# Attention's buffers move to the other side of the on-chip memory, and its first tiles are issued beside the last of the input projection

## The chip, the cores and the metric

The kernel runs on one core of one Trainium2 chip. A core has five engines, each with its own list of instructions that it runs in order: PE (TensorE, matrix products), DVE (VectorE, elementwise work and reductions), ACT (ScalarE, table functions, copies and casts), POOL (GpSimd) and SP (SyncE, which here only issues loads and stores). Engines wait for one another through semaphores, and so does SP: a load that has to wait holds up every load and store behind it in SP's list. The data lie in an on-chip memory of 128 partitions (SBUF); products are summed in a small second memory (PSUM). Everything larger lies in the chip's main memory (DRAM), and loads and stores go through 16 DMA engines.

The metric is the device time of one execution in microseconds. The kernel before takes 3681.51 us, the median of three runs from 3678.64 to 3687.2.

## The reference

The reference is a backbone of two layers over 256 context tokens and 1024 latent tokens with 1024 features each. In every layer the normed tokens go through one input projection, whose columns feed four mixers of 256 features each; the mixers' outputs are put side by side and go through one output projection onto the residual stream; then comes a feed-forward network with 4096 hidden features.

```
z   = norm(x) * (1 + scale) + shift;  z @ W_in  -> S5 | mLSTM | attention | GLA
mix = concat(S5(..), mLSTM(..), attention(..), GLA(..))
x   = x + gate * (mix @ W_out)
x   = x + gate2 * (relu(norm2(x) @ W1)**2 @ W2)
```

Attention is differential: each of the four heads has two score maps of 32 features a query, `o = softmax(q0 k0) v - lambda * softmax(q1 k1) v` with 64 features in v, and an RMS norm over o. Latent queries see all 1280 keys, context queries only the 256 of the context. The last layer needs no context outputs.

## The kernel before

Each product in float32 is done as three matmuls on rounded halves (high by high, low by high, high by low; `mm3`). So every weight that arrives (`raw`) is split by ACT (`whi`, line 1119) and DVE (`wlo`, line 1120). One layer runs in this order, by the lines of the part that builds it:

- The input projection is a generator (`rest`, tiles `zp` in PSUM, `zst` on the way out to DRAM). Its steps are traced as filler beside the S5 mixer, then beside the GLA mixer (`beside(gla, rest, 1400)`), and what is left at the end of GLA is traced in one piece (`list(rest)`). `beside(main, filler, rate)` lets the filler advance by `rate` units for each step of main. In layer 0 the steps that make the modulation vectors (`later`) follow.
- Then the pools of the projection's input and weights (`hpc`, `wpc`) are shut. `p_out` (the generator `po`) is the half of the output projection that reads the outputs of S5 and GLA: per block of 256 tokens and each of 8 groups of rows, one product of 12 matmuls (`wop`), written with the residual to a DRAM tensor `xn`.
- `da_mix` (the generator `da`) is attention. Per head it loads four tiles `daqk` of 128 x 1280 numbers, once also `davt` (v). A pair of queries' tiles gives scores (`daps`, PE, line 488); DVE takes them out of PSUM and finds the maxima (`das`, line 489); ACT takes exponentials (line 500); DVE combines the two maps (line 508); PE turns the result over (`dapt`, line 529), ACT copies it out (`dawT`) and PE multiplies by v (`dapo`, line 520). At the end of a head there is a norm (`dapr`, `dao`, `dasq`, `dams`, lines 547 to 556) and a store `mix<-dao`. A step of `da` is a score tile, a transposed group or a group of products; layer 0 has 372 steps and layer 1 has 340.
- `ml_mix` (the generator `ml`) is the mLSTM, whose gates are found by `ml_gates`: it starts with small arithmetic and short round trips through DRAM (`ml_small`, `mlsb`, `ml_rows`, `mlE`), loads q, k and v, and runs a convolution over them (`mlcy`, lines 724 to 736); then come chunks. It has about 90 steps in layer 0 and 80 in layer 1.
- The three are traced together: `beside((1 for _ in both(da, 1, ml, 0.25)), po, 0.12)`: a quarter of an mLSTM step and 0.12 products of `po` for each step of attention. Then what is left of `ml` and of `po`.
- Then the residual stream is loaded back whole (`X<-xn`, 128 x 8 x 256 numbers for the context and 128 x 8 x 512 for each half of the latent tokens), and the second half of the output projection reads the outputs of mLSTM and attention (`mr<-mix`, cast to `mh` by ACT at line 1448 and to `ml` by DVE at line 1449; again tiles `wop`), adds into X (line 1530), and the feed-forward network follows (`m1p`, `m2p`).

What sets the order is a list scheduler: it gives each engine its instructions with the traced order as priority, and the engine then runs them as they stand. Memory is handed out in pools from two ends, left and right. A tile whose place was another's before waits until that one's last reader is done. Before, `da_mix` opens its pool `dam` on the left, on the place that the projection's input and weights had, so that its first load waits for the end of the projection; the mLSTM's pools `mlg` and `ml` lie on the right, where GLA's were. The residual's pool (`X`) and the weights' pool of the second half of the output projection (`wo`) are opened on the right.

Of the kernel before, what the change touches and what calls it, by code (L numbers as in the profile page):

```python
# [452 lines left out]
def da_mix(env, l, st, V, lamv, lam_init, normg, bones, out_cb, need_ctx):  # L453

    tc, nc = env.tc, env.nc
    v, g, act, pe = nc.vector, nc.gpsimd, nc.scalar, nc.tensor
    with tc.tile_pool(name=f"dam{l}", bufs=1, reuse_waits="tile") as P:
        vt = P.tile([128, 10, 256], F32, name="davt")  # L460
        def constants():
            lv = P.tile([128, 512], F32, tag="rs_u", name="lamv", bufs=1)[:, 0:128].rearrange("p (a b) -> p a b", a=4)
            nc.sync.dma_start(lv, lamv)
            ng = P.tile([128, 1], F32, name="ng")
            nc.sync.dma_start(ng, normg)
            v.tensor_scalar(ng, ng, 1.0 - lam_init, None, op0=ALU.mult)
            lp = P.tile([128, 2, 32], F32, name="lp")
            v.tensor_tensor(lp, lv[:, 0::2, :], lv[:, 1::2, :], op=ALU.mult)
            ls = P.tile([128, 2], F32, name="ls")
            v.tensor_reduce(ls, lp, axis=AX.X, op=ALU.add)  # L470
            le = P.tile([128, 2], F32, name="le")
            exp_exact(nc, P, le, ls, 2, "le")
            nlam = P.tile([128, 1], F32, name="nlam")
            v.tensor_tensor(nlam, le[:, 1:2], le[:, 0:1], op=ALU.subtract)
            v.tensor_scalar(nlam, nlam, -lam_init, None, op0=ALU.add)
            return ng, nlam

        def scores(Q, K, qt, k1, rs):
            S, sm = {}, {}
            late_at = 2  # L480
            npc = (k1 + 511) // 512
            for m in (1, 0):
                s = S[m] = P.tile([128, T], F32, tag="s%d" % m, name="das", bufs=4 - 2 * m)
                pm = P.tile([128, 4], F32, tag="pm", name="dapm", bufs=6)
                for i in range(npc):
                    a, b = 512 * i, min(k1, 512 * i + 512)
                    p = env.bank("das2" if i == 2 else "das", "daps")
                    pe.matmul(p[:, 0:b - a], Q[m][:, 128 * qt:128 * qt + 128], K[m][:, a:b], start=True, stop=True)  # L488
                    v.tensor_scalar(s[:, a:b], p[:, 0:b - a], -1.0, None, op0=ALU.mult, op1=ALU.min, accum_out=pm[:, i:i + 1])  # L489
                    if not late_at:  # L490
                        while late:
                            late.pop(0)()
                    late_at -= 1
                    yield 1
                nm = pm
                if npc > 1:
                    nm = P.tile([128, 1], F32, tag="nm", name="danm", bufs=6)
                    v.tensor_reduce(nm, pm[:, 0:npc], axis=AX.X, op=ALU.min)  # L498
                sm[m] = P.tile([128, 1], F32, tag="sm", name="dasm", bufs=6) if m else rs
                act.activation(s[:, :k1], s[:, :k1], AF.Exp, bias=nm[:, 0:1], scale=-1.0, accum_out=sm[m])  # L500
            tiles.append(S[0])

            def combine():

                r1 = P.tile([128, 1], F32, tag="rs", name="dars", bufs=6)
                v.reciprocal(r1, sm[1])
                v.tensor_scalar(r1, r1, nlam, sm[0], op0=ALU.mult, op1=ALU.mult)
                v.scalar_tensor_tensor(S[0][:, :k1], S[1][:, :k1], r1, S[0][:, :k1], op0=ALU.mult, op1=ALU.add)
            late.append(combine)
            while len(late) > 1:  # L510
                late.pop(0)()

        def values(SS, po, h, pi, k1):

            nk = k1 // 128

            def products(i, n, wT):
                for j in range(i, i + n):
                    for z in range(2):
                        pe.matmul(po[64 * z:64 * z + 64, 128 * pi:128 * pi + 128], vt[:, j, 64 * h:64 * h + 64], wT[z][:, j - i], start=j == 0, stop=j == nk - 1)  # L520
            before = None
            for i in range(0, nk, 4):
                n = min(4, nk - i)
                wT = []
                for S in SS:
                    w = P.tile([128, 4, 128], F32, tag="wT", name="dawT", bufs=4)
                    p = env.bank("dat", "dapt")
                    for j in range(n):
                        pe.transpose(p[:, 128 * j:128 * j + 128], S[:, 128 * (i + j):128 * (i + j) + 128], env.ident)  # L529
                    act.copy(w[:, 0:n].rearrange("p a b -> p (a b)"), p[:, 0:128 * n])  # L530
                    wT.append(w)
                    yield 1
                if before:
                    products(*before)
                    yield 1
                before = (i, n, wT)
            products(*before)
            yield 1

        def finish(po, h, pairs, rs):  # L540

            n = 128 * len(pairs)
            v.reciprocal(rs[:, 0:2 * len(pairs)], rs[:, 0:2 * len(pairs)])
            pr = env.bank("dat", "dapr")
            for pi in range(len(pairs)):
                for z in range(2):
                    pe.matmul(pr[64 * z:64 * z + 64, 128 * pi:128 * pi + 128], rs[:, 2 * pi + z:2 * pi + z + 1].to_broadcast([128, 64]), env.ident, start=True, stop=True)
            o = P.tile([128, 512], F32, tag="o", name="dao", bufs=1)[:, 0:n]
            act.copy(o, pr[:, 0:n])
            v.tensor_tensor(o, o, po[:, 0:n], op=ALU.mult)  # L550
            sq = P.tile([128, 512], F32, tag="rs_u", name="dasq", bufs=1)[:, 0:n]
            act.activation(sq, o, AF.Square)
            pms = env.bank("dat", "dams")
            pe.matmul(pms[:, 0:n], bones, sq, start=True, stop=True)
            y = rstd_wide(env, P, pms[:, 0:n], n)
            v.scalar_tensor_tensor(o, o, ng, y, op0=ALU.mult, op1=ALU.mult)
            for z in range(2):
                out_cb(h, o[64 * z:64 * z + 64, 0:n], 128 * pairs[0][z])
            yield 1
        tiles, late = [], []  # L560
        todo = []

        def drain(n):
            while n and todo:
                for _ in todo[0]:
                    n -= 1
                    yield 1
                    if not n:
                        return
                todo.pop(0)  # L570
        for h in range(4):
            Qs, Ks = [], []
            for hm in (2 * h, 2 * h + 1):
                for w, L_ in ((1, Ks), (0, Qs)):
                    tl = P.tile([128, T], F32R, tag="qk%d" % w, name="daqk%d" % w, bufs=3)
                    src = st[w].rearrange("b i (j h) t -> (b i j) h t", h=8)[:, hm, :]
                    c0 = 0 if need_ctx or w == 1 else TC
                    nc.sync.dma_start(tl[:, c0:].bitcast(F32), src[:, c0:])
                    L_.append(tl)
            if h == 0:  # L580
                ng, nlam = constants()
                nc.sync.dma_start(vt, V.rearrange("(t p) c -> p t c", p=128))
            for pairs, k1 in ([([(0, 1)], TC)] if need_ctx else []) + [([(2, 6), (3, 7), (4, 8), (5, 9)], T)]:
                po = env.bank("dao", "dapo")
                rs = P.tile([128, 8], F32, tag="rk", name="dark", bufs=2)
                for pi, pr in enumerate(pairs):
                    for z in range(2):
                        yield from scores(Qs, Ks, pr[z], k1, rs[:, 2 * pi + z:2 * pi + z + 1])
                        yield from drain(5 + z)
                    todo.append(values((tiles.pop(-2), tiles.pop()), po, h, pi, k1))  # L590
                todo.append(finish(po, h, pairs, rs))
        for f in late:
            f()
        yield from drain(1000)
# [513 lines left out]
DQ = 32 ** -0.5  # L1108
HID = (2, 4)


# [158 lines left out]
def tile_hybrid_backbone(ctx: ExitStack, tc: tile.TileContext, io, out):  # L1270
# [97 lines left out]
    for l in range(L):  # L1368
# [62 lines left out]
        if l == 0:  # L1431
            list(later)
            make_scale(0, 1)
# [283 lines left out]
```

## Time and profile before

| | before |
|---|---|
| median of three runs | 3681.51 us (3678.64 to 3687.2) |
| the profiled execution | 3686.26 us, its span 3684.5 us |
| busy share of the span: PE, DVE, ACT, POOL | 92%, 60%, 36%, 12% |
| TensorE's granted clock, mean | 0.955 |
| layer 0: last store of GLA; last matmul of the projection; first score tile | 601.89; 629.9; 648.14 us |
| layer 0: last store of attention; first product that reads it | 1006.51; 1015.78 us |
| layer 1: last store of GLA; last matmul of the projection; first score tile | 2530.77; 2560.5; 2571.09 us |
| layer 1: last store of attention; first product that reads it | 2882.68; 2888.45 us |

The span is the time from the first to the last instruction of the one profiled execution. A stretch has busy times per engine; the granted clock is 1.00 at TensorE's full speed of 2.4 GHz and 0.50 at its lower level of 1.2 GHz. A row of the timeline gives start, duration, engine, line, operation and the tiles as written<-read; square brackets give how long the engine had been idle and what released it. An engine named SPq is SP issuing a load or store: the row is the issue, not the transfer.

### The profile page before, as it was taken

Reading aid. Unit: us, or ns where it says so; the run is one execution under the profiler, and the core shown is the slowest. Engines: PE = TensorE matmul, PEld = TensorE weight load, DVE = VectorE, ACT = ScalarE, POOL = GpSimd, SP = SyncE. Lnnn points to the kernel's source line nnn. Section 1 sums busy time; section 2 is a strip of 40 time slices with the busy share of each in tenths; the row PEclk is TensorE's granted clock in tenths of the full one; section 3 lists DMA queues with packets and bytes.
Section 4 is the critical chain, followed back from the end, with each engine's and each line's share of the span. In section 5 each row is a group of like instructions: output and inputs, shape, how many; then the busy total and the mean of one; then the engine's idle time right before and its main releaser. Section 6 shows DMA issues by size and latency. Waiting matters only on the chain. (4 is left out here: it accounts for less than half of the span.)

```text
span 3684.5 us, 55377 instructions
## 1 busy us (share of the span) xinstructions
PE 3393.9 (92%) x21282; PEld 2677.8 (73%) x21282; DVE 2228.0 (60%) x5455; ACT 1309.5 (36%) x2457; POOL 448.6 (12%) x520
## 2 busy tenths in 40 slices
PE   6989998898789999999999798988889899999998
PEld 3767767676657888888888476867677578888885
DVE  9664785878659855555544647486888543333334
ACT  4223434666542121212111522444776422122222
POOL 2131221223100000000000113130222000000000
PEclk8989999898899999999999898999999899999999
DMA  6775314655461222222111365314654511111112
GB/s 220 238 221 155 119 68 143 211 181 169 146 205 58 90 83 76 85 76 76 64 41 38 110 197 163 111 66 141 219 175 126 191 41 46 52 46 52 46 49 77
DMA packets 233966, 430.36 MB, mean 117 GB/s; under 512 B 47414, under 2 KB 135910, under 8 KB 233446
## 3 DMA queue, kind: packets, MB, share of 16 engines
q1 hardware_dynamic: 192806, 381.03, 31.7%
q10 hardware_dynamic: 35520, 30.52, 2.6%
q0 software_dynamic: 5376, 15.28, 1.2%
q8 instruction: 168, 2.75, 0.3%
q14 instruction: 96, 0.79, 0.1%
HBM read 316.88 MB, written 109.86 MB: 116 GB/s over the span
## 5 line engine op out<-in xcount | busy, mean ns | idle before, releaser
L1566 DVE SCALAR_TENSOR_TENSOR X<-m2p,mods,X 128x256 f32<-128x256 f32 (+1 forms) x512 | 344.9, 682 | 345.5 <-PE m2p L1130 344.9
L1119 ACT CAST whi<-raw 128x1024 fp32r<-128x1024 f32 x182 | 191.1, 1050 | 919.7 <-PE m2p L1129 640.8
L1128 PE MATMUL m2p<-hidhi,whi 128*128 128x512 f32 (+1 forms) x1280 | 473.4, 372 | 3.1 <-DVE X L1566 2.4
L1130 PE MATMUL m2p<-hidhi,wlo 128*128 128x512 f32 (+1 forms) x1280 | 472.0, 370 | 0.8 <-DVE wlo L1120 0.8
L1128 PE MATMUL m1p<-h2hi,whi 128*128 128x512 f32 (+1 forms) x1280 | 472.6, 370 | 0.2 <-ACT h2hi L1213 0.2
L1129 PE MATMUL m2p<-hidlo,whi 128*128 128x512 f32 (+1 forms) x1280 | 472.7, 369 | 0.0
L1129 PE MATMUL m1p<-h2lo,whi 128*128 128x512 f32 (+1 forms) x1280 | 471.0, 368 | 0.0
L1130 PE MATMUL m1p<-h2hi,wlo 128*128 128x512 f32 (+1 forms) x1280 | 470.9, 368 | 0.0
L1120 DVE TENSOR_TENSOR wlo<-raw,whi 128x1024 fp32r<-128x1024 f32 x182 | 224.5, 1234 | 315.2 <-ACT whi L1119 302.7
L1128 PEld LDWEIGHTS m2p<-hidhi,whi 128*128 128x128 f32 x1280 | 241.3, 189 | 60.4 <-issue 9.4
L1128 PEld LDWEIGHTS m1p<-h2hi,whi 128*128 128x128 f32 x1280 | 241.0, 188 | 46.5 <-ACT whi L1119 4.2
L1130 PEld LDWEIGHTS m2p<-hidhi,wlo 128*128 128x128 f32 x1280 | 241.0, 188 | 46.4 <-issue 3.4
L1129 PEld LDWEIGHTS m2p<-hidlo,whi 128*128 128x128 f32 x1280 | 241.4, 189 | 41.8 <-issue 2.2
L1129 PEld LDWEIGHTS m1p<-h2lo,whi 128*128 128x128 f32 x1280 | 241.2, 188 | 40.6 <-DVE h2lo L1214 0.6
L1130 PEld LDWEIGHTS m1p<-h2hi,wlo 128*128 128x128 f32 x1280 | 241.0, 188 | 40.2 <-issue 0.4
L1128 PE MATMUL zp<-hhi,whi 128*128 128x512 f32 (+1 forms) x664 | 254.5, 384 | 11.3 <-ACT zst L1241 9.6
L1129 PE MATMUL zp<-hlo,whi 128*128 128x512 f32 (+1 forms) x664 | 251.4, 379 | 8.6 <-DVE hlo L1209 8.2
L489 DVE TENSOR_SCALAR_CACHE_REDUCE das<-daps 128x512 f32<-128x512 f32 (+1 forms) x400 | 225.8, 587 | 45.5 <-PE daps L488 42.9
L1130 PE MATMUL zp<-hhi,wlo 128*128 128x512 f32 (+1 forms) x664 | 250.0, 377 | 0.0
L1580 DVE TENSOR_TENSOR rl<-rl,m1p 128x256 f32<-128x256 f32 (+1 forms) x160 | 100.6, 629 | 172.2 <-ACT rl L1579 172.1
L500 ACT ACTIVATE das<-das,danm 128x1280 f32<-128x1280 f32 x128 | 174.3, 1362 | 48.1 <-DVE danm L498 47.9
L488 PE MATMUL daps<-daqk,daqk 128*128 128x512 f32 (+1 forms) x400 | 149.7, 438 | 41.3 <-DVE das L489 39.8
(460 smaller groups left out, 6571.9 us busy)
## 6 DMA issues: line engine op xcount, KB each, us to landing
raw<-w SPq DMA_DIRECT2D x136, 512.0 KB
adaw<-ada_w SPq DMA_DIRECT2D x96, 512.0 KB
whl<-wsp SPq DMA_DIRECT2D x80, 512.0 KB
wsp<-whl SPq DMA_DIRECT2D x32, 512.0 KB
raw<-wz SPq DMA_DIRECT2D x30, 512.0 KB
daqk<-da_st SPq DMA_DIRECT2D x24, 640.0 KB
mlE<-ml_rows SPq DMA_DIRECT2D x16, 640.0 KB
xn<-xo SPq DMA_DIRECT2D x72, 128.0 KB
```

The source lines that it names most:

```text
L488: pe.matmul(p[:, 0:b - a], Q[m][:, 128 * qt:128 * qt + 128], K[m][:, a:b], start=True, stop=True)
L489: v.tensor_scalar(s[:, a:b], p[:, 0:b - a], -1.0, None, op0=ALU.mult, op1=ALU.min, accum_out=pm[:, i:i + 1])
L500: act.activation(s[:, :k1], s[:, :k1], AF.Exp, bias=nm[:, 0:1], scale=-1.0, accum_out=sm[m])
L1119: nc.scalar.copy(hi, raw)
L1120: nc.vector.tensor_tensor(lo, raw, hi.bitcast(F32), op=ALU.subtract)
L1128: pe.matmul(out, ah, bh, start=i == 0, stop=False)
L1129: pe.matmul(out, ah, bl, start=False, stop=False)
L1130: pe.matmul(out, al, bh, start=False, stop=i == n - 1)
L1566: nc.vector.scalar_tensor_tensor(X[b][:, m], p[:, :n], mod(l, 5, s)[:, m:m + 1], X[b][:, m], op0=ALU.mult, op1=ALU.add)
L1580: nc.vector.tensor_tensor(rl[:, :n], rl[:, :n], p[:, :n], op=ALU.mult)
```

## The change

Attention's pool is handed to `da_mix` by its caller, which opens it on the right as soon as GLA has ended, before the projection is. The PSUM banks are swapped at that point too. The first 28 (layer 0) or 24 (layer 1) steps of attention are traced beside what is left of the projection, and the rest as before beside mLSTM and `po`. The body of `da_mix` is otherwise only moved to the left by one level. In layer 0 the remaining steps of `later` and `make_scale` are traced ahead of this.

```
-def da_mix(env, l, st, V, lamv, lam_init, normg, bones, out_cb, need_ctx):
+def da_mix(env, l, P, st, V, lamv, lam_init, normg, bones, out_cb, need_ctx):
-    with tc.tile_pool(name=f"dam{l}", bufs=1, reuse_waits="tile") as P:
...
+EARLY = (28, 24)
...
         beside(gla, rest, 1400)
-        list(rest)
+
         if l == 0:
             list(later)
             make_scale(0, 1)
+        shut(ps2c)
+        ps2c = banks(f"psd{l}")
+        env.banks.update(mls="m", mlv="m", wo="b", dat="b")
+        damc, P = pool(f"dam{l}", "right")
+        da = da_mix(env, l, P, st, zd["dav"], io["da_lam"][l], 0.8 - 0.6 * math.exp(-0.3 * l), io["da_ng"][l], env.bones, put_da, need)
+        beside((1 for _ in itertools.islice(da, EARLY[l])), rest, 1200)
+        list(rest)
         shut(hpc)
         shut(wpc)
...
-        shut(ps2c)
-        ps2c = banks(f"psd{l}")
-        env.banks.update(mls="m", mlv="m", wo="b", dat="b")
         wpc, env.wp = pool("wpd")
         env.whl = 2
         poc, P = pool(f"po{l}")
         po = p_out(P)
-        da = da_mix(env, l, st, zd["dav"], io["da_lam"][l], 0.8 - 0.6 * math.exp(-0.3 * l), io["da_ng"][l], env.bones, put_da, need)
         mgc, MG = pool(f"mlg{l}", "right")
...
         beside((1 for _ in both(da, 1, ml, 0.25)), po, 0.12)
         list(ml)
         shut(mgc)
+        shut(damc)
         list(po)
```

So the right end now holds attention's tiles at the bottom and the mLSTM's above them, and after both the residual's and the weights' pools take that place.

PE in layer 0, where the projection ends (before). `zp` is the projection, `mlpt` and `mlpu` are the mLSTM, `daps` is attention:

```order
2319 L1129 MATMUL zp<-wlo,hhi_379 128x256
2320 L1130 MATMUL zp<-whi,hlo_380 128x256
2321 L674 MATMUL mlpt<-ident,ig 128x104
2322 L675 MATMUL mlpt<-ident,mlbb 128x104
2323 L683 MATMUL mlpt<-mlam,mle 128x40
2324 L758 MATMUL mlpt<-ident,mlkT 128x128 x10
2325 L790 MATMUL mlpu<-mlvx,mlkw 64x65
2326 L488 MATMUL daps<-daqk_6204,daqk_6206 128x256
```

The same engine in the changed kernel, from the first score tile on:

```order
2175 L1130 MATMUL zp<-wlo,hhi_377 128x256
2176 L488 MATMUL daps<-daqk_5702,daqk_5704 128x256
2177 L488 MATMUL daps<-daqk_5698,daqk_5700 128x256
2178 L488 MATMUL daps<-daqk_5702,daqk_5704 128x256
2179 L1131 MATMUL zp<-whi,hlo_378 128x256
2180 L1129 MATMUL zp<-whi,hhi_377 128x256
2181 L1130 MATMUL zp<-wlo,hhi_377 128x256
2182 L488 MATMUL daps<-daqk_5702,daqk_5704 128x256
2183 L1131 MATMUL zp<-whi,hlo_378 128x256
```

The score tiles have moved ahead of the last 145 matmuls of the projection and in between them; the mLSTM's `mlpt` now come after the projection and after attention's first tiles. On DVE the same is to be seen: the mLSTM's gates and convolution (before 51 rows between the last `wlo` and the first `das`) come after three whole tiles of attention.

SP in layer 0 at the end of attention (before). `X` is the residual stream, `mr` and `raw` feed the second half of the output projection, `mix<-dao` is attention's last store:

```order
350 L869 DMA mlog<-z_mlo_116 128x2x128
351 L1518 DMA X_10839<-xn_6098 128x8x256
352 L1518 DMA X_10843<-xn_6098 128x8x512
353 L1518 DMA X_10847<-xn_6098 128x8x512
354 L1447 DMA mr<-mix_102 128x512 x2
355 L1459 DMA raw<-wo 128x512 x2
356 L1447 DMA mr<-mix_102 128x512
357 L1462 DMA wsp_6101<-whl 128x1024 x2
358 L1414 DMA mix_102<-dao 64x512 x2
359 L1459 DMA raw<-wo 128x512 x2
360 L1447 DMA mr<-mix_102 128x512 x2
```

And in the changed kernel:

```order
352 L869 DMA mlog<-z_mlo_116 128x2x128
353 L1494 DMA xn_6333<-xo 128x256
354 L1415 DMA mix_102<-dao 64x512 x2
355 L1523 DMA X_10839<-xn_6333 128x8x256
356 L1523 DMA X_10843<-xn_6333 128x8x512
357 L1523 DMA X_10847<-xn_6333 128x8x512
358 L1455 DMA mr<-mix_102 128x512 x2
359 L1467 DMA raw<-wo 128x512 x2
```

The three loads of the residual and everything behind them have moved from ahead of attention's last store to behind it. Layer 1 in the changed kernel:

```order
715 L1117 DMA raw<-w 128x1024 x2
716 L1415 DMA mix_19843<-dao 64x512 x2
717 L1117 DMA raw<-w 128x1024 x2
718 L1523 DMA X_28017<-xn_24106 128x8x512
719 L1523 DMA X_28021<-xn_24106 128x8x512
720 L1455 DMA mr<-mix_19843 128x512 x2
721 L1467 DMA raw<-wo 128x512 x2
```

There four loads of the feed-forward weights stand ahead of X as well (before, X was the first of them all, and the four weights came after `mr`).

## Rows read from the trace of the kernel before

**Rows 1.** The page, busy time of the span: us (share), number of instructions.

```profile
PE 3393.9 (92%) x21282; PEld 2677.8 (73%) x21282; DVE 2228.0 (60%) x5455; ACT 1309.5 (36%) x2457; POOL 448.6 (12%) x520
```

**Rows 2.** Busy times by stretch, layer 0; the head names the columns.

```profile
core 0: us, PE busy (x) PEld busy (x) DVE busy (x) ACT busy (x) POOL busy (x), PEclk, DMA share, GB/s
602.00:614.00 12.00, 12.00 (x102) 12.00 (x101) 6.35 (x17) 3.57 (x6) 0.99 (x14) 1.00 0.62 150
614.00:632.00 18.00, 16.49 (x139) 16.37 (x137) 12.70 (x23) 11.94 (x13) 0.19 (x3) 1.00 0.85 219
632.00:658.00 26.00, 6.33 (x19) 3.58 (x19) 20.53 (x53) 19.28 (x43) 4.30 (x3) 0.55 0.78 264
658.00:700.00 42.00, 35.36 (x200) 26.76 (x201) 36.53 (x106) 31.72 (x75) 7.29 (x6) 0.79 0.68 221
700.00:950.00 250.00, 227.50 (x2062) 178.60 (x2061) 200.50 (x679) 164.06 (x367) 63.34 (x61) 0.95 0.54 173
```

**Rows 3.** Busy times by stretch, layer 1.

```profile
2531.00:2543.00 12.00, 11.04 (x87) 10.46 (x86) 7.07 (x15) 4.65 (x7) 0.83 (x12) 1.00 0.64 198
2543.00:2620.00 77.00, 59.06 (x360) 47.58 (x358) 61.90 (x166) 60.02 (x119) 12.52 (x11) 0.80 0.73 238
```

**Rows 4.** Timeline of PE, layer 0, between the projection's end and attention's second tile.

```profile
647.76 0.45 PE L790 MATMUL mlpu<-mlvx,mlkw 128*64 128x65 f32 x2 [10.88 <-issue]
...
658.56 0.80 PE L488 MATMUL daps<-daqk,daqk 128*128 128x512 f32 x1 [6.36 <-DVE das L489]
```

**Rows 5.** Timeline of SP's queue, layer 0, GLA's last store and attention's first loads.

```profile
601.89 0.32 SPq L1410 DMA_DIRECT2D mix<-glsq  x1
...
632.42 2.49 SPq L578 DMA_DIRECT2D daqk<-da_st  x4
```

**Rows 6.** Timeline of PE, first and last matmul of one of `po`'s products.

```profile
703.79 0.39 PE L1128 MATMUL wop<-mh,whl 128*128 128x256 f32 x1
...
705.20 0.28 PE L1130 MATMUL wop<-mh,whl 128*128 128x256 f32 x1
```

**Rows 7.** Timeline of SP's queue, layer 0, end of attention.

```profile
973.62 3.05 SPq L1518 DMA_DIRECT2D X<-xn  x3
...
1001.41 0.33 SPq L1447 DMA_DIRECT2D mr<-mix  x1
...
1006.51 1.12 SPq L1414 DMA_DIRECT2D mix<-dao  x2
...
1008.80 0.93 SPq L1447 DMA_DIRECT2D mr<-mix  x2
```

**Rows 8.** Busy times by stretch, while X is loaded, layer 0.

```profile
980.00:990.00 10.00, 6.37 (x46) 4.47 (x45) 7.45 (x27) 6.03 (x15) 2.46 (x2) 0.80 1.05 386
```

**Rows 9.** Timeline of ACT, layer 0, the casts of two pieces of `mr`.

```profile
1004.12 0.62 ACT L1448 CAST mh<-mr 128x512 fp32r<-128x512 f32 x1 [0.87 <-DMA mr<-mix]
1015.11 0.62 ACT L1448 CAST mh<-mr 128x512 fp32r<-128x512 f32 x1 [10.37 <-DMA mr<-mix]
```

**Rows 10.** Timeline of PE, layer 0, the first 18 products of the second half and the next.

```profile
1002.78 0.79 PE L1128 MATMUL wop<-mh,whl 128*128 128x512 f32 x1 [3.36 <-ACT whl L1460]
...
1015.78 0.80 PE L1128 MATMUL wop<-mh,whl 128*128 128x512 f32 x1 [6.89 <-ACT mh L1448]
```

**Rows 11.** Timeline of SP's queue, layer 1, end of attention.

```profile
2847.30 2.67 SPq L1518 DMA_DIRECT2D X<-xn  x2
...
2882.68 1.13 SPq L1414 DMA_DIRECT2D mix<-dao  x2
```

**Rows 12.** Timeline of PE, layer 1, products of the second half and their two stalls.

```profile
2879.76 0.39 PE L1130 MATMUL wop<-mh,whl 128*128 128x512 f32 x1
2888.45 0.80 PE L1128 MATMUL wop<-mh,whl 128*128 128x512 f32 x1 [8.30 <-ACT mh L1448]
...
2893.71 0.80 PE L1128 MATMUL wop<-mh,whl 128*128 128x512 f32 x1 [2.03 <-ACT whl L1460]
```

More of the change, by code (lines that the diff above doesn't have):

```diff
@@ L4 @@
 import contextlib
+import itertools
 from concourse import mybir
@@ L450, in da_prep, with da_mix @@
                 yield 1
-def da_mix(env, l, st, V, lamv, lam_init, normg, bones, out_cb, need_ctx):
+def da_mix(env, l, P, st, V, lamv, lam_init, normg, bones, out_cb, need_ctx):
     tc, nc = env.tc, env.nc
     v, g, act, pe = nc.vector, nc.gpsimd, nc.scalar, nc.tensor
[L459 to L545, printed above, removed]
-                for z in range(2):
[L547 to L556, printed above, removed]
-            for z in range(2):
[L558 to L594, printed above, removed]
@@ new lines, in values, with products @@
+    def values(SS, po, h, pi, k1):
+        nk = k1 // 128
+        def products(i, n, wT):
+            for j in range(i, i + n):
+                for z in range(2):
+                    pe.matmul(po[64 * z:64 * z + 64, 128 * pi:128 * pi + 128], vt[:, j, 64 * h:64 * h + 64], wT[z][:, j - i], start=j == 0, stop=j == nk - 1)
+        before = None
+        for i in range(0, nk, 4):
+            n = min(4, nk - i)
+            wT = []
+            for S in SS:
+                w = P.tile([128, 4, 128], F32, tag="wT", name="dawT", bufs=4)
+                p = env.bank("dat", "dapt")
+                for j in range(n):
+                    pe.transpose(p[:, 128 * j:128 * j + 128], S[:, 128 * (i + j):128 * (i + j) + 128], env.ident)
+                act.copy(w[:, 0:n].rearrange("p a b -> p (a b)"), p[:, 0:128 * n])
+                wT.append(w)
+                yield 1
+            if before:
+                products(*before)
+                yield 1
+            before = (i, n, wT)
+        products(*before)
+        yield 1
@@ L597, in silu_parts @@
+    for f in late:
+        f()
+    yield from drain(1000)
 def silu_parts(env, P, sg, x):
@@ L1108 @@
 DQ = 32 ** -0.5
+EARLY = (28, 24)
 HID = (2, 4)
@@ L1429, in tile_hybrid_backbone @@
         beside(gla, rest, 1400)
-        list(rest)
         if l == 0:
@@ L1433, in tile_hybrid_backbone @@
             make_scale(0, 1)
+        shut(ps2c)
+        ps2c = banks(f"psd{l}")
+        env.banks.update(mls="m", mlv="m", wo="b", dat="b")
+        damc, P = pool(f"dam{l}", "right")
+        da = da_mix(env, l, P, st, zd["dav"], io["da_lam"][l], 0.8 - 0.6 * math.exp(-0.3 * l), io["da_ng"][l], env.bones, put_da, need)
+        beside((1 for _ in itertools.islice(da, EARLY[l])), rest, 1200)
+        list(rest)
         shut(hpc)
```

103 lines of the change are left out of this document (99 added, 4 removed).

## The prediction

> **What bounds the kernel now.** I began with the busy times of the page: PE is busy 92% of the span and every other engine 60% or less [rows 1], so a change pays only where PE stands idle or runs at its lower clock. Then I cut the two places that the diff touches into stretches. From GLA's last store to the steady part of attention, layer 0 has 98 us (602 to 700) in which PE is busy 12.00 + 16.49 + 6.33 + 35.36 = 70.2, so 27.8 idle, and in the worst of it (632 to 658) the granted clock is 0.55, most of it at the lower of the two levels [rows 2]. In layer 1 it is 70.1 of 89, so 18.9 idle [rows 3]. The timeline of PE then says what it waits for: 10.88 us before `mlpu` and 6.36 us before the second score tile, the latter for DVE [rows 4]. Attention's loads go out at 632.42, 30.5 us after GLA's last store at 601.89 [rows 5], because their place in memory is the projection's. That is the hole that the change fills. The end of attention is the second place: there PE waits for `mr`, the piece of attention's output that has to come back from DRAM [rows 10, 12].
>
> **Hand-over from projection to attention.** The list of PE shows score tiles between the last 145 matmuls of the projection, so PE is no longer without work when it ends. But DVE's work isn't less: attention's first tiles come earlier and the mLSTM's gates and convolution, which DVE did beside the projection, come later, since their place is now where the projection's input lies. So I count DVE. In 602 to 700 it does 6.35 + 12.70 + 20.53 + 36.53 = 76.1 us of work [rows 2]. Afterwards the first score tile waits for four loads of 128 x 1280 x 4 bytes, 2.6 MB; at the 219 to 264 GB/s of this stretch these are 10 to 12 us, to about 614. Up to there DVE has only the projection's share, which I put at half of 6.35, as the mLSTM's instructions go out of it. The other 73 us are done at some density. The nearest row, DVE beside attention from 658 to 700, is 36.53 of 42 or 0.87; the most is 1.00. I take 0.93, between them, since the 10.9 us that DVE idled in 602 to 632 can now be filled: 614 + 73/0.93 = 692.5 in place of 700, 7.5 us won. Ends: 13 us at density 1.00; at the 200.5/250 = 0.80 of the steady part [rows 2] it is 705, 5 us lost. In layer 1: 7.07 + 61.90 = 69.0 us of DVE work [rows 3], 3.5 up to 2543, 65.5/0.93 = 70.4, so 2613.4 in place of 2620, 6.6 us won (ends 11.5 won, 5 lost). Together 14. Above both stands what PE can win at most, its idle 27.8 and 18.9 us, if DVE's work could be put off into the steady part, where it is busy 80%.
>
> **Filler.** The 28 and 24 early steps take no products of `po` along. At 0.12 for a step 3.4 and 2.9 products move towards the end of attention, where before there was no filler left. Twelve matmuls take 703.79 to 705.20 and one pace more [rows 6], some 1.44 us: 4.8 + 4.1 = 9 us, if PE is idle where they land. Ends 0 and 9; I take 9, because PE waits in that tail.
>
> **End of attention, layer 0.** Here the change adds a wait. X, 1.05 + 2.1 + 2.1 = 5.24 MB, was issued at 973.62, 33 us ahead of attention's last store at 1006.51 [rows 7], and moved under attention at 386 GB/s [rows 8]. Now X lies on attention's own tiles, waits for the last transposes and products, and stands behind that store in SP's list; behind it stand all of `mr` and `raw`. Let S be the issue of the last store. X goes out at S + 1.1 (the store's own 1.12 us), takes 5.24/386 GB/s = 13.6 us, to S + 15.1 with 0.4 for its start. Two pieces of `mr` of 0.26 MB follow: an unhindered one was issued at 1001.41 and cast at 1004.12, 2.7 us [rows 7, 9], and the second adds 0.7: S + 18.5. From the cast to the product it is 1015.78 - 1015.11 = 0.67 [rows 9, 10], so the products run from S + 19.2 instead of S + 9.3 (1015.78 - 1006.51): 9.9 us. On top, the 18 products that filled 1002.78 to 1008.89 now also come after X; they need 18 x 0.235 = 4.2 us at the full clock. The loss is 14 us. Ends: 8, if `mr` passes through beside X so that only half of its transfer counts (9.9 - 6.8 + 4.2 = 7.3); 20, if the low clock after the long idle and the weights behind `mr` add what the 18 products cost in this trace (6.1).
>
> A page of the Trainium skill decides between those ends. The trace shows 2.7 us for an `mr` with little ahead of it and 1015.11 - 1008.80 = 6.3 us for one that followed attention's last store at once [rows 7, 9], so `mr` waits for what went ahead. The Trainium skill, "DMA: Bandwidth & Descriptors", section "Queues, rings and completion order", says that SP has one ring on each of the 16 DMA engines and that each takes its descriptors in ring order; by that rule `mr` starts behind the whole of X, and the loss is the 14 us of the sum. If the transfers shared the engines evenly it would be the 7.
>
> **End of attention, layer 1.** X is 4.2 MB, issued 35 us ahead of the last store before [rows 11]. Afterwards 2 of the 0.52 MB weights and X stand behind the store: 5.24 MB again, 13.6 us, to S + 15.1, `mr` at S + 18.5, the product at S + 19.2 instead of 2888.45 - 2882.68 = S + 5.8: 13.4. Some 20 products that ran ahead of 2880.15 come later, 4.7 us, and the stall of 2.03 for weights [rows 12] goes, as these are now in: 16 us lost. Ends 7 and 20, by the same reasons.
>
> **Sum.** -14 - 9 + 14 + 16 = +7 us. The profiled execution is 3686.26 us, of which 1.8 lie outside the span; by it the changed kernel would take 3693. The profile stands 4.75 us above the median of the runs, 3681.51, so I forecast 3688.
>
> **The rivals.**
> - Faster. PE sets the pace of the hand-over and DVE's late work is absorbed in its 20% of free time from 700 to 950 [rows 2]. What stalls PE is then gone to two thirds: 18 + 13 = 31, with the filler 40, against 30 lost: 3671. For it: PE has filler of two kinds there. Against it: DVE is at 9 tenths right after the hand-over, and `das` waits on it in order.
> - No change. X's transfer hides in part under the norm that attention's last head still needs, or shares the engines with `mr`: 10 + 12 lost, 23 won: 3680.5. Against it: X stands behind the store that ends this very norm.
> - Slower by more. The mLSTM starts some 40 us later, and its convolution and round trips now stand in DVE's list between attention's score tiles. The 16.4 us that DVE idled in 602 to 658 [rows 2] come again, this time with `das` queued behind them and PE behind that. The hand-over then wins nothing, and the mLSTM, whose last instructions now stand behind attention's in PE's list, ends after it: +5 in each layer (an estimate, half of such a wait in one layer). 30 + 10 - 9 = +31, less what of the old hole is filled anyway (some 8): 3704. It decides as soon as DVE waits for more than the 14 us that I count as won.
> - The change doesn't do what it says: the four loads come in late, with the DMA engines at 0.85 from 614 to 632 [rows 2], and the early tiles run only when the projection has ended. Won 9, lost 30: 3702.
>
> **How the numbers follow.** The forecast has 0.42, faster 0.28, no change 0.10, slower by more 0.14, late loads 0.06. A measurement of this kernel can tell 0.2% (7.4 us, so 3674 and 3689) from no change. The forecast's own range is 3681 to 3697, with somewhat more than half of it above 3689. So slower is 0.14 + 0.06 + 0.23 = 0.43, the same 0.10 + 0.19 = 0.29, faster 0.28. For 8 in 10 the range goes down to 3666, into the first rival (its own upper end, all of the hole filled, would be some 3655), and up to 3706, past the last two.
>
> **What would show it.** Right: the first `daps` of layer 0 some 14 us after GLA's last store, no idle of PE over 5 us around the projection's end, and DVE at 0.9 or more from there to about 690. At the end of attention SP issues X right behind `mix<-dao`, DMA at some 386 GB/s for 13 us with PE idle, and the first product that reads `mr` 19 us after that store. Wrong: if PE is at work within 12 us of that store, the loss is halved and the kernel is as fast as before or faster; if the steady part of attention begins 20 us earlier than now, the first rival holds; if PE waits for DVE behind `mlcy` again and again, the third.

## The result and the profile after

The changed kernel takes 3737.99 us (3736.6 to 3740.96), against 3680.07 for the kernel before on the same chip: a ratio of 1.0155 with a 95% interval of 1.0137 to 1.0172, some 57 us slower. The forecast was 3688, with a range from 3666 to 3706; the measured time lies outside it.

Its page has the busy times almost where they were [rows 1]: 12 us more for PE, 19 more for DVE, in a span that is 50.3 us longer.

```profile
span 3734.8 us, 55372 instructions
...
PE 3406.1 (91%) x21282; PEld 2688.5 (72%) x21282; DVE 2246.6 (60%) x5455; ACT 1311.5 (35%) x2457; POOL 450.2 (12%) x520
```

So the work is the same, and PE stands idle some 38 us longer. To find where, I cut each layer at three events: the `glms` matmul of GLA (the first of layer 0 and the last of layer 1), the issue S of attention's last store, and the first matmul `m1p` of the feed-forward network. A is from `glms` to S, B from S to `m1p`. The view of `glms` gives the first cut: count, least, median and largest duration in ns, first and last start. Before:

```profile
L1076 PE MATMUL glms<-glsq,bones x20: 379/593/992, 491.4 to 2523.2; 128*128 128x512 f32 x16, 128*128 128x256 f32 x4
```

After:

```profile
L1076 PE MATMUL glms<-glsq,bones x20: 379/592/697, 488.4 to 2548.2; 128*128 128x512 f32 x16, 128*128 128x256 f32 x4
```

S was at 1006.51 and 2882.68 [rows 7, 11] and is at 1018.38 and 2916.49 (below). All runs of this study, in us, from one profile each; A of the same instructions differs by 6 to 9 us from profile to profile (the changed kernel and the run e2_x_late are the same up to S), so only larger differences count in one row:

| run | A, layer 0 | B, layer 0 | A, layer 1 | B, layer 1 | median | against before, 95% |
|---|---|---|---|---|---|---|
| before | 515 | 98 | 360 | 73 | 3681.5 | |
| changed | 530 | 116 | 368 | 90 | 3738.0 | 1.0137 to 1.0172 |
| e1 no early steps | 527 | 118 | 374 | 85 | 3737.0 | 1.0124 to 1.0160 |
| e2 `mr` ahead of X | 536 | 110 | 377 | 87 | 3745.8 | 1.0140 to 1.0180 |
| e3 before, both later | 526 | 108 | 370 | 76 | 3714.9 | 1.0057 to 1.0096 |
| e4 mLSTM 0.30 | 530 | 114 | 367 | 85 | 3728.7 | 1.0098 to 1.0138 |
| f1 before, po later | 525 | 96 | 381 | 71 | 3708.1 | 1.0044 to 1.0075 |
| f2 before, mLSTM later | 519 | 108 | 364 | 75 | 3706.0 | 1.0034 to 1.0066 |
| f3 0.30 and 0.14 | 524 | 114 | 377 | 85 | 3736.5 | 1.0120 to 1.0151 |
| f5 no load of X | 534 | 108 | 378 | 78 | 3729.9 | 1.0091 to 1.0131 |
| f7 before, po sooner | 540 | 98 | 392 | 69 | 3737.4 | 1.0119 to 1.0153 |
| g1 before, no mLSTM | 439 | 99 | 307 | 73 | 3549.5 | 0.9612 to 0.9651 |
| g2 changed, no mLSTM | 432 | 114 | 289 | 85 | 3552.1 | 0.9625 to 0.9655 |
| g4 no load of X, 0.30 | 529 | 103 | 359 | 74 | 3698.3 | 1.0025 to 1.0057 |
| h1 half the early steps | 540 | 118 | 366 | 86 | 3750.7 | 1.0157 to 1.0190 |
| h2 changed, po 0.10 | 498 | 124 | 359 | 88 | 3707.5 | 1.0046 to 1.0092 |
| h3 before, po 0.14 | 533 | 98 | 364 | 73 | 3707.9 | 1.0038 to 1.0068 |
| h4 before, mLSTM 0.28 | 525 | 96 | 375 | 72 | 3708.9 | 1.0041 to 1.0071 |
| k1 before, po 0.10 | 517 | 103 | 361 | 72 | 3695.4 | 1.0020 to 1.0055 |
| k2 changed, 0.30 and 0.10 | 522 | 122 | 379 | 84 | 3742.6 | 1.0152 to 1.0204 |

The changed kernel loses 15 + 9 us in A and 18 + 16 in B; the rest of the span is 8 us shorter in this pair of profiles. (The 9 alone would be within what one profile can tell; e2, with the same instructions there, has 18.)

**Part B** went as foreseen. SP's queue at the end of layer 0 and of layer 1 in the changed kernel (start, duration, engine, line, operation):

```profile
1018.38 1.09 SPq L1415 DMA_DIRECT2D mix<-dao  x2
1019.57 3.71 SPq L1523 DMA_DIRECT2D X<-xn  x3
1023.33 5.58 SPq L1455 DMA_DIRECT2D mr<-mix  x2
...
2916.49 1.09 SPq L1415 DMA_DIRECT2D mix<-dao  x2
...
2919.32 1.43 SPq L1523 DMA_DIRECT2D X<-xn  x2
```

PE there, in layer 0 and layer 1:

```profile
1040.00 0.79 PE L1129 MATMUL wop<-mh,whl 128*128 128x512 f32 x1 [19.49 <-ACT whl L1468]
...
2938.16 0.80 PE L1129 MATMUL wop<-mh,whl 128*128 128x512 f32 x1 [26.51 <-ACT whl L1468]
```

X stands right behind the last store (in layer 1 with two loads of weights in between), and the first product comes 21.6 us and 21.7 us after it, where 9.3 and 5.8 stood before [rows 7, 10 to 12]. In layer 0 the first `mr` behind X is cast 19.6 us after the store:

```profile
1037.97 1.31 ACT L1456 CAST mh<-mr 128x512 fp32r<-128x512 f32 x2 [17.06 <-DMA mr<-mix]
```

In between PE is at the lower clock (0.50) and the DMA engines are full:

```profile
1019.00:1042.00 23.00, 2.69 (x7) 1.86 (x8) 3.33 (x7) 2.84 (x5) 0.01 (x1) 0.50 0.97 338
```

**Part A** did not. Attention's loads go out as soon as GLA has ended, 30 us sooner than before, counted from GLA's last store [rows 5], and the first score tile comes 10.7 us after that store (14 were foreseen):

```profile
597.00 0.32 SPq L1411 DMA_DIRECT2D mix<-glsq  x1
597.42 2.01 SPq L578 DMA_DIRECT2D daqk<-da_st  x4
```

The score matmuls of layer 0 alone, by stretches of 40 us (columns PE, PEld and DVE, each busy time and count; then clock, DMA share, GB/s). Before:

```profile
600.00:640.00 40.00, 0.00 (x0) 0.00 (x0) 0.00 (x0) 0.93 0.77 211
640.00:680.00 40.00, 11.14 (x25) 5.87 (x25) 13.42 (x48) 0.67 0.67 230
680.00:720.00 40.00, 10.19 (x26) 4.66 (x26) 14.41 (x51) 0.89 0.60 193
720.00:760.00 40.00, 8.28 (x24) 4.04 (x24) 13.11 (x49) 0.96 0.72 230
```

After:

```profile
600.00:640.00 40.00, 10.05 (x29) 5.26 (x29) 14.97 (x53) 0.99 0.54 187
640.00:680.00 40.00, 6.44 (x14) 2.77 (x14) 7.35 (x26) 0.71 0.64 181
680.00:720.00 40.00, 6.95 (x14) 3.64 (x14) 7.74 (x28) 0.66 0.74 248
720.00:760.00 40.00, 10.12 (x21) 4.47 (x21) 12.82 (x46) 0.85 0.51 149
```

A head start of 29 score matmuls at 640 is down to 57 against 51 at 720 and 78 against 75 at 760. From 640 to 740 DVE does this in the changed kernel (groups by shape: count, busy us, mean ns, idle before):

```profile
L489 DVE TENSOR_SCALAR_CACHE_REDUCE das<-daps 128x512 f32<-128x512 f32 x23 | 15.5, 684 | 2.3 <-PE daps L488 1.1 <-PE dapt L529 1.0
...
L725 DVE SCALAR_TENSOR_TENSOR mlcy<-mlzp,mlcw,mlcy 128x1281 f32<-128x1281 f32 x4 | 6.7, 1676 | 0.0
L726 DVE SCALAR_TENSOR_TENSOR mlcy<-mlzp,mlcw,mlcy 128x1281 f32<-128x1281 f32 x4 | 6.5, 1615 | 0.0
...
L771 DVE TENSOR_TENSOR mlkw<-mlkn,mlE 128x640 f32<-128x640 f32 x4 | 5.2, 1299 | 0.0
```

The mLSTM's convolution (`mlcy`) and its weighting of k (`mlkw`) stand there. Before, five of these eight `mlcy` instructions of layer 0 began while the projection still ran (612.0 to 628.7; its last matmul came at 629.9) and three in the hole behind it; `mlkw` stood among attention's tiles before, too (646.8 to 693.6). All engines, 50 us at a time from GLA's last store on, show what that does (columns as in the prediction's rows). Before:

```profile
602.00:652.00 50.00, 34.62 (x258) 31.95 (x256) 33.88 (x72) 33.17 (x58) 2.59 (x19) 0.82 0.84 245
652.00:702.00 50.00, 37.56 (x221) 28.36 (x222) 44.22 (x130) 34.93 (x81) 11.28 (x8) 0.77 0.59 193
702.00:752.00 50.00, 47.38 (x435) 37.49 (x434) 38.23 (x131) 29.46 (x62) 12.24 (x10) 0.97 0.67 216
```

After:

```profile
597.00:647.00 50.00, 44.17 (x324) 39.13 (x322) 34.35 (x129) 21.83 (x44) 1.19 (x14) 0.92 0.57 185
647.00:697.00 50.00, 32.22 (x165) 24.26 (x163) 43.13 (x91) 40.45 (x71) 9.00 (x9) 0.70 0.68 206
697.00:747.00 50.00, 42.92 (x334) 32.06 (x334) 35.73 (x102) 34.76 (x83) 11.09 (x10) 0.86 0.69 217
```

In the first stretch PE does 66 matmuls more than before, in the second 56 fewer, in the third 101 fewer. The hole has not gone; it has moved 50 us down and become wider.

DVE, on whose count the forecast rested, wins next to nothing. From the first score tile to 692.5 it is busy 71.89 of 84.50 us, a density of 0.85; before, it was 0.81 from 614 to 700 [rows 2]. From GLA's last store it needs 98.6 us for the 76.1 us of work that took 98 before [rows 2], and in layer 1 87 us for the 69 that took 89 [rows 3]:

```profile
608.00:692.50 84.50, 62.70 (x382) 50.74 (x380) 71.89 (x207) 57.20 (x101) 9.54 (x19) 0.80 0.58 178
597.00:695.60 98.60, 75.19 (x485) 62.92 (x483) 76.08 (x218) 60.89 (x111) 9.98 (x22) 0.82 0.62 194
...
2556.00:2643.00 87.00, 68.78 (x463) 57.28 (x461) 69.16 (x195) 56.96 (x98) 7.39 (x20) 0.90 0.69 212
```

### The profile page after: what moved, and what is told of

It reads as the page before. It is cut to its first block, busy times and chain, and to the rows that moved or that the text cites. A ratio compares the mean times of both kernels' runs of the same rounds, so it can differ in the third digit from the quotient of the medians.

```text
span 3734.8 us, 55372 instructions
## 1 busy us (share of the span) xinstructions
PE 3406.1 (91%) x21282; PEld 2688.5 (72%) x21282; DVE 2246.6 (60%) x5455; ACT 1311.5 (35%) x2457; POOL 450.2 (12%) x520
## 5 line engine op out<-in xcount | busy, mean ns | idle before, releaser
L1129 PE MATMUL wop<-mh,whl 128*128 128x256 f32 (+1 forms) x448 | 160.9, 361 | 65.6 <-ACT whl L1468 54.6
L488 PE MATMUL daps<-daqk,daqk 128*128 128x512 f32 (+1 forms) x400 | 157.8, 449 | 50.0 <-DVE das L489 45.9
```

The source lines that it names most:

```text
L1129: pe.matmul(out, ah, bh, start=i == 0, stop=False)
```

## The experiments

**Which part of the change.** e1 is the changed kernel without early steps.

```
-EARLY = (28, 24)
+EARLY = (0, 0)
```

> The changed kernel with no early steps (0 and 0 instead of 28 and 24); attention's memory stays on the right, the mLSTM's above it. Theory A (the attention stage is longer because the mLSTM's preparation, which ran beside the projection, now has to wait for the projection's end and runs among attention's tiles; the end is longer because the residual's loads stand behind attention's last store): the early tiles are a help that is eaten up, without them it is as slow or slower, 3735 to 3755. Rival B (the early tiles themselves cost: they break up the projection's dense matmuls and push fillers about): the attention stage returns to its old length and only the end's 34 us stay, 3705 to 3718.

Measured 3737.0, as with them. So the rest of the change (the place in memory, and with it the earlier swap of the PSUM banks and the order of `later`) costs as much by itself, and the early steps neither win nor lose on top of it at these rates.

e3 is the kernel before, with memory as it was; f1 and f2 hold back only one of the two.

```
 e3: +        for _ in range((28, 24)[l]):
     +            next(da)
 f1: +        par = both(da, 1, ml, 0.25)
     +        for _ in range((28, 24)[l]):
     +            next(par)
     +        beside((1 for _ in par), po, 0.12)
 f2: +        beside((1 for _ in itertools.islice(da, (28, 24)[l])), po, 0.12)
```

> The kernel before, with memory as it was, but the first 28 and 24 steps of attention traced alone, before the mLSTM and po go beside the rest. Theory A (what hurts is that the mLSTM and po come later, wherever the tiles lie): 10 to 25 us slower than before, 3690 to 3705. Rival D (what hurts is the place in memory, which keeps the mLSTM's preparation from running beside the projection): within 5 us of before, 3675 to 3685.

> The kernel before, with its memory, but po's products are withheld for the first 28 and 24 steps of attention; the mLSTM goes beside all of them. Theory E (of the 30 us that the later mLSTM and po cost together, the filler is the larger part, since PE is idle at the hand-over and busy later): 10 to 20 us slower than before, 3692 to 3705. Rival F (the mLSTM's later start is the larger part): within 7 us of before.

> The kernel before, with its memory, but the mLSTM's steps are withheld for the first 28 and 24 steps of attention; po goes beside all of them. Theory E: within 10 us of before, 3680 to 3694. Rival F: 15 to 30 us slower than before, 3698 to 3714, with the mLSTM's last block after attention's.

e3 is 28 us slower than before (0.77%), more than the 10 to 25 of its theory A; f1 is 22 slower (0.60%) and f2 18 (0.50%); both E and F had expected one of these two near zero, and both miss. Holding back some six of `po`'s products, 9 us of matmuls by [rows 6], costs more than twice their own time, all of it in A; holding back the mLSTM costs mostly in B of layer 0 (10 us).

**The end of attention.** e2 loads X in pieces behind `mr`; e4 hurries the mLSTM; f5 has POOL set X to a constant instead of loading it, so that the residual is left out; g4 does that in small pieces and hurries the mLSTM.

```
 e2: -            nc.sync.dma_start(X[b], xn_d[:, :, BLK[b][0]:BLK[b][1]])
     ...
     +                if i == 0:
     +                    nc.sync.dma_start(X[b][:, m], xn_d[:, m, BLK[b][0]:BLK[b][1]])
     +                if m == 2 and i + 1 < len(LAST[l]):
     +                    bx = LAST[l][i + 1]
     +                    nc.sync.dma_start(X[bx], xn_d[:, :, BLK[bx][0]:BLK[bx][1]])
 e4: both(da, 1, ml, 0.3)
 f5: -            nc.sync.dma_start(X[b], xn_d[:, :, BLK[b][0]:BLK[b][1]])
     +            nc.gpsimd.memset(X[b], 0.5)
 g4: -            nc.sync.dma_start(X[b], xn_d[:, :, BLK[b][0]:BLK[b][1]])
     ...
     +                nc.gpsimd.memset(X[b][:, m], 0.5)   and both(da, 1, ml, 0.3)
```

> The changed kernel, but the residual's first block is loaded row group by row group after the pieces of mr, and the other blocks later, so that mr no longer waits behind 5.24 and 4.2 MB. Theory A: 10 us less in layer 0 and 8 to 13 less in layer 1, 3712 to 3720. Rival C (the end is longer for another reason, the mLSTM that ends after attention or the cold clock): no more than 5 us less, 3733 or above.

> The changed kernel with 0.30 mLSTM steps for each attention step in place of 0.25, so that the mLSTM is through before attention ends. Theory A with the late mLSTM as the larger part: 8 to 20 us less, 3718 to 3730. If the hand-over is the larger part: within 5 us of the changed kernel, 3733 to 3743.

> The changed kernel without the loads of the residual in front of the second half of the output projection (POOL sets X to a constant instead, so the residual up to there is left out). Theory G (the end of each layer's attention is longer by the bytes of X, which now move in a stretch that the DMA engines already fill): 24 to 36 us below the changed kernel, 3702 to 3716, the stretch from attention's last store to the first m1p back at 98 to 103 us in layer 0. Rival C (the mLSTM that ends late, or the clock after the idle): less than 12 us below.

> The changed kernel without the loads of X (set to a constant by POOL piece by piece after attention, so the residual up to there is left out) and with 0.30 mLSTM steps for each attention step. Theory J (attention's end is longer for two reasons, each enough for most of it: the bytes of X behind the last store, and the mLSTM's last block, which lets 18 products of the second half start late): both gone, the first product after attention's last store comes after 9 to 13 us in layer 0 and 6 to 10 in layer 1, and the total is 30 to 40 us below the changed kernel, 3698 to 3708. If only the attention stage matters: no lower than 3722.

e2 is no faster (3745.8), where its theory A had 3712 to 3720: B is 6 and 2 us shorter, and its longer A lies within what one profile can tell. It brought the first cast of `mr` after the last store forward, from 19.6 to 4.8 us behind it in layer 0, but the bytes of X still move through full DMA engines (a busy share of 0.80 to 0.99 in each 10 us from 1027 to 1077), and the products wait further on. e4 wins 9 to 14 us, at the low end of its expectation. f5 is 8 us below the changed kernel by the medians and 16 by the ratios, short of the 24 to 36 of theory G (rival C had less than 12); in it POOL's writing of X held up DVE ahead of the last store (last section), so it doesn't decide. g4 has no such hold-up, though its first eight pieces are written some 13 us before the last store of layer 0: the instruction of DVE that was held up in f5 takes 0.43 us there. It takes 3698.3, with B at 103 and 74, almost before's 98 and 73. SP and PE of g4 in layer 0:

```profile
1017.61 1.09 SPq L1415 DMA_DIRECT2D mix<-dao  x2
...
1019.38 0.99 SPq L1455 DMA_DIRECT2D mr<-mix  x2
```

```profile
1027.00 0.79 PE L1129 MATMUL wop<-mh,whl 128*128 128x512 f32 x1 [8.41 <-ACT whl L1468]
```

The first product is 9.4 us after the last store, as before (9.3). Against e4, which differs in X alone, B is 11 + 11 us shorter: that is X. Of the 18 + 16 us lost in B, X is 11 + 11, the mLSTM's higher rate saves 2 + 5 (e4 against the changed kernel), and 4 us in layer 0 are left. That the mLSTM ends late is the smaller part: in e1 it ends 11 and 15 us before the last store, and B is 118 and 85 all the same.

**The mLSTM.** g1 and g2 are the kernel before and the changed one without it.

```
-        mgates = ml_gates(...)
-        ml = ml_mix(...)
+        zero = MG.tile([128, T], F32, name="zero")
+        nc.gpsimd.memset(zero, 0.0)
+        for hp in range(2):
+            put(1)(hp, zero, 0)
+        ml = iter(())
```

> The kernel before without the mLSTM (its gates, convolution and chunks are left out, zeros are stored as its output). A base for the next run: from GLA's last store to attention's last copy it should be 20 to 80 us shorter than the kernel before in the two layers together.

> The changed kernel without the mLSTM, to be read against the run above. Theory H (the early tiles are won, and the mLSTM's preparation, which the change pushes behind the projection, takes it all back): attention's stage is 10 to 20 us shorter in each layer than above, and the loads of X give back 11 to 14 us in each, so the total is within 15 us of it or below it. Rival I (the early tiles win nothing, whether the mLSTM is there or not): attention's stage is as long as above or longer, and the total is 25 to 40 us above it.

g2 takes 3552.1 against g1's 3549.5: without the mLSTM the 57 us are 2.5, inside the intervals. A is 7 and 17 us shorter by the change, B 14 and 11 longer. (The two runs leave out the whole mLSTM, not its preparation alone.) g1's two A are 129 us shorter than before's, where 20 to 80 were expected: the mLSTM is dearer than I thought. The end of layer 0 in g1:

```profile
929.06 1.10 SPq L1414 DMA_DIRECT2D mix<-dao  x2
931.33 0.80 SPq L1447 DMA_DIRECT2D mr<-mix  x2
```

And in g2, where attention's last store comes 10 us sooner and X stands behind it:

```profile
918.62 1.09 SPq L1415 DMA_DIRECT2D mix<-dao  x2
...
920.38 5.09 SPq L1525 DMA_DIRECT2D X<-xn  x3
925.52 5.08 SPq L1455 DMA_DIRECT2D mr<-mix  x2
```

**The rhythm.** The other runs change only how many mLSTM steps and products of `po` fall to a step of attention, or how many steps are early.

```
 f3: changed  both(da, 1, ml, 0.3)),  po, 0.14      h2: changed  po, 0.1
 k2: changed  both(da, 1, ml, 0.3)),  po, 0.1       h1: changed  EARLY = (14, 12)
 h3: before   po, 0.14      k1: before  po, 0.1     h4: before   both(da, 1, ml, 0.28)
 f7: before   +  par = both(da, 1, ml, 0.25)
              +  beside((1 for _ in itertools.islice(par, 28)), po, 0.3)
              +  beside((1 for _ in par), po, 0.12)
```

> The changed kernel with 0.30 mLSTM steps and 0.14 products of po for each attention step, so that both are through as early as before. If the filler's lateness costs (theory E): 15 to 25 us below the changed kernel, 3713 to 3723, and 5 to 15 below the one with 0.30 alone. If not: as that one, 3725 to 3733. Either way it stays well above the kernel before, since the residual's loads and the mLSTM's preparation are where they were.

> The kernel before with 0.30 products of po for each of the first 28 steps (attention and mLSTM as they were) and 0.12 after. If what po's absence costs there (23 us in the run that withheld it) can also be had the other way round: 5 to 20 us faster than before, 3664 to 3680. If the hand-over has no more room: the same or slower, 3680 to 3700.

> The changed kernel with half the early steps (14 and 12). Theory H (the mLSTM's preparation, displaced from beside the projection, costs 24 us in each layer however many tiles come early; 0 and 28 steps gave the same time): 3730 to 3745 again. Theory K (the loss lies in the rhythm in which mLSTM and po fall among attention's steps, and another rhythm would not have it): 10 or more away from both, in either direction.

> The changed kernel with 0.10 products of po for each step in place of 0.12. Theory H: 3730 to 3750. Theory K: 10 or more us away from the changed kernel's 3738, in either direction.

> The kernel before with 0.14 products of po for each step in place of 0.12: memory and the place of everything else are as they were. Theory K: such a small change of rhythm alone costs 10 to 30 us, 3695 to 3715, as both withholding po for the first steps (23) and hurrying it there (52) did. If the rhythm matters only at the hand-over: within 8 us of before.

> The kernel before with 0.28 mLSTM steps for each attention step in place of 0.25. Theory K: 10 to 30 us slower than before, 3695 to 3715. If the rhythm matters little: within 8 us of before.

> The kernel before with 0.10 products of po for each step in place of 0.12, the control to the changed kernel at 0.10 (3707). If 0.10 is the better rhythm in itself, it helps here as well: 3655 to 3675. If each arrangement has a rhythm of its own (theory K) and before's is 0.12: 3695 to 3710, as at 0.14. If the rhythm matters only with early tiles: within 8 us of before.

> The changed kernel with 0.10 products of po and 0.30 mLSTM steps for each step. If the two act each by itself: 31 less from po and 9 less from the mLSTM than the changed kernel, 3695 to 3702. If the rhythm of all three together decides (theory K): anywhere from 3700 to 3740, and not the sum.

Theory K, that the loss hangs on the rhythm of the three streams, is borne out by most of these runs. With memory untouched, every rate tried beside 0.25 and 0.12 makes the kernel before slower: by 12 us (k1), 20 (h3, h4) and 50 (f7, where more of `po` was to fill the hole and neither expectation held). The changed kernel gains 31 us by 0.10 in place of 0.12 (h2), and loses all of it again with 0.30 for the mLSTM on top (k2, which had 3695 to 3702 if the rates added up, and is 3 us above theory K's range as well). f3, which hurries both, is as slow as the changed kernel, where 3713 to 3733 was expected. With half the early steps (h1) the kernel is 13 us slower than with all by the medians, but 7 by the ratios, whose intervals meet; so h1 doesn't decide between H and K. No run with all of the work was faster than the kernel before.

At 0.10 for both, the change costs 1.0069 against 1.0037 (h2, k1), about 12 us, though the two intervals meet. In this pair the parts are near the forecast's: by the change A is 19 and 2 us shorter, and B 20 and 16 longer. (28 matmuls of `po`, under 4 us by [rows 6], have moved from A to B in h2.) So with the mLSTM in place the same change costs 24 us in A at one rate and wins 21 at another, by one profile each, while its loss in B stays. Nor does the hole after GLA set A by itself. h2 has nearly the same one, 843 matmuls in the three stretches of 50 us, against 823 in the changed kernel and 914 before, and yet its A of layer 0 is 32 us shorter than the changed kernel's:

```profile
598.00:648.00 50.00, 44.32 (x323) 39.20 (x324) 34.18 (x129) 22.01 (x45) 1.76 (x15) 0.92 0.57 183
648.00:698.00 50.00, 35.20 (x174) 25.24 (x172) 48.07 (x95) 42.15 (x78) 11.85 (x9) 0.67 0.74 220
698.00:748.00 50.00, 44.21 (x346) 34.07 (x346) 39.08 (x121) 37.79 (x87) 12.28 (x9) 0.86 0.64 207
```

What a rhythm does is spread over two things. Attention's stage of layer 0 before, from GLA's last store to the last turn of a tile:

```profile
602.00:994.00 392.00, 333.91 (x2817) 265.07 (x2817) 306.30 (x983) 255.02 (x552) 84.23 (x95) 0.89 0.58 184
```

In the changed kernel:

```profile
597.00:1006.00 409.00, 345.31 (x2764) 272.83 (x2764) 310.73 (x964) 253.19 (x544) 83.23 (x91) 0.87 0.51 161
```

And in h2:

```profile
598.00:974.00 376.00, 329.98 (x2697) 259.49 (x2698) 302.38 (x964) 250.39 (x540) 78.50 (x87) 0.88 0.52 166
```

PE is idle for 58, 64 and 46 us of them, and busy for 334, 345 and 330; the granted clock is 0.89, 0.87 and 0.88. The work is the same, but for 52 matmuls of the mLSTM, which in the changed kernel and in h2 come after the last turn of a tile, and 67 of `po`, which do so in h2. The 208 score matmuls, the same in all, are busy for 76.5 us before and 86.5 in the changed kernel. So the difference is partly waits and partly matmuls that take longer. The largest wait among them is that of the score matmuls for DVE to empty PSUM (us in all, times, longest), before, changed and h2 in this order:

```profile
PE daps L488 <- DVE das L489: 24.4, 20, 6.4
```

```profile
PE daps L488 <- DVE das L489: 35.8, 28, 7.6
```

```profile
PE daps L488 <- DVE das L489: 13.6, 15, 2.2
```

## Why the prediction was wrong

- **The end of attention** was right in mechanism and nearly in size: 14 + 16 us foreseen, 18 + 16 measured in B. The first cast of `mr` was put at 18.5 us after the last store and came after 19.6, behind X; the first product was put at 19.2 and came after 21.6 and 21.7. X alone accounts for 11 + 11 (g4 against e4). The 18 products that ran from 1002.78 on in layer 0 before [rows 10] now come behind the last store, as foreseen; they do so in e4 and g4 too, where the mLSTM ends 35 us before that store, so its late end is not what holds them back. That the order of X and `mr` decides, as the two ends of this term had it, did not show in the total: e2 turned it round and won nothing. (The low end is given as 8 and once as 7; its sum is 7.3.)
- **The hand-over** is the step that failed: "So I count DVE", the 73 us of its work at a density of 0.93, 7.5 and 6.6 us won, and the filler's 9 us on top: 23 won, where A lost 15 + 9. Two things in it were wrong. First, the density was 0.85 in layer 0, so that DVE was through with the counted work no sooner than before there, and 2 us sooner in layer 1, in place of 14 together. Second, the rest of the stage was taken as given from there on. It isn't: it hangs on how the mLSTM and `po` fall among attention's steps, and the sum had no term for that. At the kernel's own rates A is 15 and 9 us longer by the change, at 0.10 19 and 2 shorter, without the mLSTM 7 and 17 shorter. The last two sums, 21 and 24, are close to the forecast's 23, but not layer by layer, and they come from other kernels than the one that was forecast (without the mLSTM part of the work that was counted is gone). As far as these runs show, that closeness is luck.
- **The filler** was counted as 9 us won. f1 held back as much of it with nothing else changed and lost 22 us. (By [rows 6] a product takes 1.41 us and a pace of 0.12, 1.53 and not 1.44; that is 0.6 us in all.)
- **The rivals.** The third had the mechanism that the trace of the changed kernel shows, at 14% and 3704: DVE's work among the score tiles, a hand-over that wins nothing, the mLSTM ending after attention (it does so in layer 0, by 2 us). Its price, nothing won and 5 us in each layer, left the total 34 us short. "The change doesn't do what it says" is out: the loads go out 0.4 us after GLA's last store. The first, that DVE's free time from 700 on would absorb its late work, is out too at these rates: A grew.
- **What stays open.** How much of the loss in A is the displaced preparation and how much the rhythm cannot be told apart: e1 has the old rhythm with the preparation displaced and is as slow, but h2 has it displaced as well and its A of layer 0 is shorter than before's. A rhythm fits one arrangement and not the next, and why 0.10 fits this one was not found. An arrangement with the mLSTM's preparation still beside the projection and attention's early tiles too has not been tried; attention's pool alone takes some 85 KB per partition by the sizes of its tiles.

## What to carry to other kernels

When a buffer is moved so that one stage can start early, ask whose place is taken: the stage that now has to wait may have been the one whose work was free where it ran. Where three streams share engines that run in order, rates tuned for one arrangement are part of it: compare arrangements each at several rates (here 12 to 31 us lay between neighbouring rates), and leave a stream out of both kernels to see what a change is worth without it. A forecast that prices only the hand-over takes the rest of the stage as fixed; here one step in one rate moved it by 41 us in the two layers (h2 against the changed kernel). A load that moves behind the last store of a stage can cost the time of its bytes where the transfers are full already; here it did so whichever load went first.

## What the hardware showed that I had not expected

In f5 POOL wrote X (5.25 us for two pieces of 128 x 2048, from 1012.42) while DVE was in the norm of attention's last head. POOL, then DVE:

```profile
1012.42 5.25 POOL L1523 MEMSET X<- 128x2048 f32 x2
```

```profile
1012.05 5.90 DVE L49 TENSOR_SCALAR rs_u<-rs_u 128x512 f32<-128x512 f32 x1
```

That DVE instruction takes 0.42 us in the kernel before (line 48 there) and 5.90 beside the writing, and it ended 0.3 us after it. In layer 1 of f5 one of only 128 x 4 numbers takes 3.79 us (from 2911.03) beside a writing of 3.51. The changed kernel has milder meetings of its own: at 745.79 and 748.82 two instructions of attention's norm take 2.76 and 3.02 us beside POOL's `mlab` (744.94, two in 6.35 us), and 0.69 and 0.74 in the kernel before. Taking a load away by having POOL write the tile is therefore no clean experiment where DVE is on the path; in g4, in small pieces that met none of attention's norm, it was.
